# Tap matrices read from memory instead of built, and low weight parts made one stage earlier

## The chip, the cores and the metric

The kernel runs on one core of a Trainium2 chip. The metric is the device time of one execution in microseconds (us); a kernel's time is the median of several runs.

## The reference, cut to what matters

Two layers on a stream of 512 latent tokens of width 1024 (256 context tokens feed the first layer only). Layer 0 mixes tokens with gated linear attention, layer 1 with a convolution module; a SwiGLU block follows each.

```python
u = h @ w_in                                    # swiglu, hidden width 2816
y = (silu(u[..., :2816]) * u[..., 2816:]) @ w_out

u = h @ w_pw1 + b_pw1                           # conv_module: 1024 -> 2048
u = u[..., :1024] * sigmoid(u[..., 1024:])
u = depthwise_conv(u, w_dw) + b_dw              # 31 taps per channel
u = silu(layernorm(u, ln_g, ln_b))
y = u @ w_pw2 + b_pw2
```

Every sub-layer sees `rmsnorm(x) * (1 + scale) + shift`, and `x = x + gate * y` follows; the six vectors of a layer are `silu(c) @ w_mod[i] + b_mod[i]`.

## The kernel before

Activations lie with features on the 128 partitions and tokens along the free dimension, so a 1024-wide stream is 8 tiles of 128 x 512. Float32 products are made of three passes: a number is split in a high part (a cast to fp32r, on ScalarE) and a low part (the difference, on VectorE), and `mm3` adds high*high, high*low and low*high in PSUM. A weight block of 128 x 1024 arrives in a tile `wr` (3 buffers) from the SP queue, its high part goes to `wh` (4 buffers, L110) and its low part to `wl` (4 buffers, L111).

Activation tiles of 2 KB per partition come from a pool with a fixed number of buffers for each tag: `x` 8, `h` 16, `s` 36, `c` 4, `d` 4, `t` 3, `g` 4. A tile asked for by `bt(tag)` takes a buffer of its tag when an earlier tile of the tag has had its last reader.

The stages around the change, in order of time:

- The first feed-forward block, `ffn(0, ...)`. Its first product (`pairs`, 22 pairs of weight blocks) reads the 16 `h` tiles of its input. `evac` writes the 22 hidden blocks as high and low tiles: 36 `s`, 4 `c` and 4 `d`.

```python
tag = "s" if j < 18 else "c" if j < 20 else "d"
sT.append((bt(tag, F32R), bt(tag, F32R)))
```

- Its second product (`out_proj`) runs over 8 output blocks `m`, the last one in two halves of 256 tokens, and reads all 44 hidden tiles for each. After each half, `after2` calls `in2`: the norm of the half (`rstd_y`, `newton`, `spread`) and, for each of 8 feature blocks, `modulate`, which writes the 16 `h` tiles of the convolution's input.
- Beside the first product run jobs (`mod_jobs`, called by `step(n)`) that make the modulation vectors: load a block of `w_mod` into `wm` (one buffer), multiply and sum on VectorE (L229), add a bias on GpSimd (L233).
- The convolution module. `toeplitz` first builds 27 tap tiles on GpSimd (L1128) for three feature blocks (`PCH`) whose taps run on TensorE. Then 8 pairs of products (`pair_mm`, weights by `pair_load`) alternate with the taps: three lanes in an order written out by hand put taps on VectorE (L1088), on GpSimd with ScalarE (L1046, L1047) and on TensorE (L1152). The order of the SP queue is not written by hand.
- The second pointwise product, then the second feed-forward block.

Of the kernel before, what the change touches and what calls it, by code (L numbers as in the profile page):

```python
# [7 lines left out]
F32 = mybir.dt.float32  # L8
F32R = mybir.dt.float32r
# [7 lines left out]
ALU = mybir.AluOpType  # L17

P = 128
# [36 lines left out]
def hybrid_kernel(ctx: ExitStack, tc: tile.TileContext, t: dict):  # L56
# [29 lines left out]
    def bt(tag, dt=F32):  # L86
        if tag in "cd":
            return wide(tag, dt)[:, 2:514]
        return big.tile([P, 512], dt, tag=tag, bufs=NBUF[tag], name=nm(tag))
# [14 lines left out]
    def load_w(ap, n=1024, lo_eng=dve):  # L104
        return hilo(load_raw(ap, n), n, lo_eng)
# [111 lines left out]
    def mod_jobs():  # L217

        ij = [(0, j) for j in range(16, 48)] + [(1, j) for j in range(48)]

        def load(i, j):
            raw = wts.tile([P, 1024], F32, tag="wm", bufs=1, name=nm("wm"))
            sp.dma_start(raw, t["wmod"][i, j])
            return raw
        raw = load(*ij[0])
        yield
        for n, (i, j) in enumerate(ij):
            o = i * 48 + j
            dve.scalar_tensor_tensor(raw, raw, 1.0, sil, op0=ALU.mult, op1=ALU.mult, accum_out=dots[:, o:o + 1])  # L229
            if n + 1 < len(ij):  # L230
                raw = load(*ij[n + 1])
            if j % 8 == 7:
                pool.tensor_tensor(mod[i][:, j - 7:j + 1], dots[:, o - 7:o + 1],  # L233
                                   col(C_BMOD + o - 7, 8), op=ALU.add)
            yield

# [2 lines left out]
    def step(n):  # L239
        for _ in range(n):  # L240
            if next(jobs, 0) == 0:
                return
# [695 lines left out]
            if beside:  # L938
                beside(i)

    def ffn(i, h_, gt2, nx, after):
        sT = []

        def evac(j, po, c0, c1):
            n = c1 - c0
            if c0 == 0:
                tag = "s" if j < 18 else "c" if j < 20 else "d"
                sT.append((bt(tag, F32R), bt(tag, F32R)))
            hi, lo = sT[j]
            a = bt("t")  # L950
            act.activation(a[:, :n], po[0][:, :n], AF.Silu)
            dve.tensor_tensor(a[:, :n], a[:, :n], po[1][:, :n], op=ALU.mult)  # L952
            act.copy(hi[:, c0:c1], a[:, :n])  # L953
            dve.tensor_tensor(lo[:, c0:c1], a[:, :n], hi[:, c0:c1].bitcast(F32), op=ALU.subtract)

        pairs(f"wf{i}", HC, h_, evac, lambda i: step(3))
        r = resid(gt2)

        def ev2(m, p_, c0, c1):
            r(m, p_, c0, c1)  # L960
            nx.add(m, xs[m], c0, c1)

        out_proj(f"wo{i}", HC, sT, ev2, nx.tail, after)

# [14 lines left out]

    def after2(hf):  # L980
        if hf == 0:
            step(100)
            make_a(acol[:, 24:32], mod[1][:, 8:16], col(C_GMIX + 8, 8))
            make_a(acol[:, 32:40], mod[1][:, 32:40], col(C_GFFN + 8, 8))
        in2(hf)

    ffn(0, in1.h, mod[0][:, 40:48], n2, after2)


    HALF = WID // 2  # L990
# [128 lines left out]

    toep, ug, pe_ps, scr = {}, {}, {}, {}  # L1120

    def toeplitz(m, tag="s"):

        c = (m - PCH[0]) * 4 * NSH * NF
        for i in range(0, 4 * NSH, 4):
            tt = bt(tag)
            w = wph[:, c + i * NF:c + (i + 4) * NF]
            pool.tensor_tensor(tt.rearrange("p (a b) -> p a b", b=32), m32.unsqueeze(1).to_broadcast([P, 16, 32]),  # L1128
                               w.unsqueeze(2).to_broadcast([P, 16, 32]), op=ALU.mult)
            for j in range(4):  # L1130
                toep[m, (i + j) // NSH, (i + j) % NSH] = tt[:, j * P:(j + 1) * P]

# [171 lines left out]
        return r  # L1304

    def pair_load(i):
        return [load_w(t["wp1"][2 * i]), load_w(t["wp1"][2 * i + 1])]

    def pair_mm(u, c0, c1, ks=range(KC), po=None):
        po = po or [ps(), ps()]  # L1310
# [6 lines left out]
    def bias2(k):  # L1317
        act.activation(xs[k], xs[k], AF.Identity, bias=gb2[:, k:k + 1])
# [32 lines left out]
            ev3(m, p_, *halves[hf])  # L1351

    ev3 = closing(mod[1][:, 16:24], n3)
    m32 = cst.tile([P, 32], F32, name="m32")
    sp.dma_start(m32, t["m32"])
    bph = cst.tile([P, 4 * len(PCH)], F32, name="bph")
    sp.dma_start(bph, t["bph"])
    wph = bt("g")
    sp.dma_start(wph[:, :len(PCH) * 4 * NSH * NF], t["wph"])
    for m in range(KC):  # L1360
        if m in PCH:
            toeplitz(m)
        else:
            cv_new(m)
    uw = {0: pair_load(0), 1: pair_load(1)}
    prod = wts.tile([P, 1024], F32, tag="wm", bufs=1, name=nm("wm"))
# [2 lines left out]
    with tc.manual_schedule(engines={E.Activation, E.DVE, E.Pool, E.PE}):  # L1369
        pool_lane = pool_order()  # L1370
        dve_start, dve_lane = dve_order()
        warm(AF.Sigmoid)
        po.update({(i, h): pair_mm(uw[i], *h) for h, i in ((h0, 0), (h0, 1), (h1, 0))})
        evc(0, po[0, h0], *h0)
        mix(dve_start[0],
            at=[(0.4, lambda: evc(1, po[1, h0], *h0)), (0.7, lambda: uw.update({2: pair_load(2)}))])
        evc(0, po[0, h1], *h1)
        po[1, h1] = pair_mm(uw[1], *h1)
        po[2] = pair_mm(uw[2], 0, SEQ)
        mix(take(pool_lane, 5), dve_start[1], at=[(0.7, lambda: evc(1, po[1, h1], *h1))])  # L1380
        for p in range(1, 7):
            def evac():
                if p > 1:
                    need(ORD[p])
                    po[ORD[p + 1]] = pair_mm(uw[p + 1], 0, SEQ, range(4))

            def second():
                if p > 1:
                    pair_mm(uw[p + 1], 0, SEQ, range(4, KC), po[ORD[p + 1]])

            def load():
                if p + 2 < KC:
                    uw[p + 2] = pair_load(ORD[p + 2])
            at = [(0.04, evac), (0.25, load), (0.5, second)]
            if p >= 3:
                at += [(0.6, lambda: bias2(2 * p - 6)), (0.8, lambda: bias2(2 * p - 5))]
            if p == 3:
                at += [(SH[0], shift_sums), (SH[1], shift_bc), (SH[2], shift_copy)]
            if p >= 5:
                at += [(0.3, lambda: to_groups(ORD[p]))]  # L1400
            mix(take(pool_lane, PN[p - 1]), take(dve_lane, DN[p - 1]), at=at)
        mix(pe_lane(4), take(pool_lane, PN[6]), take(dve_lane, DN[6]),
            at=[(N6, lambda: need(6)), (N6, lambda: to_groups(6)), (0.3, lambda: load2(0)), (0.7, lambda: load2(1))])
        pe_store(4)
        mix(pe_lane(5), take(pool_lane, PN[7]), take(dve_lane, DN[7]),
            at=[(0.3, lambda: load2(4, "s")), (0.9, lambda: pe_back(4, dve))])
        pe_store(5)
        warm(AF.Silu)
        mix(pe_lane(6), pool_lane, dve_lane, at=[(0.1, lambda: load2(2)), (0.2, lambda: load2(3))])
        cv_new(6)  # L1410
        pe_out(6, 0, act)
        pe_out(6, 1, act)
        pool.tensor_tensor(cv[6][0:64], cv[6][0:64], ncb[0:64], op=ALU.add)
        ln_open()
        pe_out(6, 2, dve)
        pe_out(6, 3, dve)
        pe_back(5, act)
        ks = (1, 0, 2, 3, 4, 7, 5, 6)
        for k in ks:
            run(ln_sums(k, 0, k == ks[-1]))  # L1420
        b = [f for k in ks for f in ln_sums(k, 1, k == ks[-1])]
        run(take(b, S1))
        ln_stat(0)
        ln_bc(0)
        run(take(b, S2))
        lane = ln_lane(0)
        run(take(lane, 5))

        def rest():
            run(b)  # L1430
            run(lane)
            ln_stat(1)
        first = pw2(range(4), 0, {1: rest, BC: lambda: ln_bc(1)})
        load2(5, "s")
        lane = ln_lane(1)
        run(take(lane, L1))
        pw2_out(first, 0)
        run(lane)
        pw2_out(pw2((4, 5), 0), 0)
        pw2_out(pw2(range(4), 1), 1)  # L1440
        load2(6)
        load2(7)
        pw2_out(pw2((4, 5), 1), 1)
# [16 lines left out]
            (sp, act)[k // 2 % 2].dma_start(t["out"][k:k + 2, :, c0:c1].rearrange("k p c -> p k c"),  # L1460
                                            y.rearrange("p (k c) -> p k c", k=2))

    ffn(1, in3.h, mod[1][:, 40:48], n4, final)

# [14 lines left out]
def phases(w):  # L1481

    import numpy as np
    pad = NF * MID + NF - 1 - WID // 2
    wp = np.pad(w, ((pad, pad), (0, 0)))
    r, d, f = np.ogrid[:NF, :NSH, :NF]
    a = wp[NF * d + r - f + NF - 1].reshape(NF, NSH, NF, KC, 4, 32)[:, :, :, list(PCH)]
    return np.ascontiguousarray(a.transpose(0, 5, 3, 4, 1, 2)).reshape(P, -1)


def layout(x, c, ctx, c_ctx, w_mod, b_mod, norm_mix_g, norm_ffn_g, gla_w_in, gla_wa_f, gla_ba_f,
# [26 lines left out]
    tt = np.arange(512)  # L1518
    a["pmask"] = np.ascontiguousarray((np.arange(P)[:, None] > (tt % P)[None]).astype(f32))
    a["ident"] = np.eye(P, dtype=f32)  # L1520
    a["m32"] = np.ascontiguousarray(np.tile(np.eye(32, dtype=f32), (4, 1)))
    b = conv_b_dw[0].reshape(KC, 4, 32)[list(PCH)].reshape(-1, 32).T
    a["bph"] = np.ascontiguousarray(np.tile(b, (NF, 1)))
    a["wph"] = phases(conv_w_dw[0])
    a["wgo"] = _units(gla_w_out[0])
    a["wp1"] = _pairs(conv_w_pw1[0])
    a["wp2"] = _units(conv_w_pw2[0])
# [21 lines left out]
```

## Time and profile before

| | us |
|---|---|
| median of 3 runs | 1287.11 (1284.47 to 1287.29) |
| the profiled execution | 1287.67 |
| its span, from the first to the last instruction | 1285.7 |

The profile shows the one profiled execution. Times in it are counted from the start of the span. Busy time is that of instructions on an engine; TensorE's matmuls are pipelined, so their durations overlap. The granted clock is the share of TensorE's full speed that it had.

### The profile page before, as it was taken

Reading aid. Unit: us, or ns where it says so; the run is one execution under the profiler, and the core shown is the slowest. Engines: PE = TensorE matmul, PEld = TensorE weight load, DVE = VectorE, ACT = ScalarE, POOL = GpSimd, SP = SyncE. Lnnn points to the kernel's source line nnn. Section 1 sums busy time; section 2 is a strip of 40 time slices with the busy share of each in tenths; the row PEclk is TensorE's granted clock in tenths of the full one; section 3 lists DMA queues with packets and bytes.
Section 4 is the critical chain, followed back from the end, with each engine's and each line's share of the span. In section 5 each row is a group of like instructions: output and inputs, shape, how many; then the busy total and the mean of one; then the engine's idle time right before and its main releaser. Section 6 shows DMA issues by size and latency. Waiting matters only on the chain.

```text
span 1285.7 us, 17000 instructions
## 1 busy us (share of the span) xinstructions
PE 1234.1 (96%) x6692; PEld 1069.6 (83%) x6692; DVE 734.7 (57%) x1279; ACT 475.8 (37%) x748; POOL 226.9 (18%) x191
## 2 busy tenths in 40 slices
PE   8899899999899999999999699999999999999997
PEld 7678799898898888877888598889988888888886
DVE  2997976747775545545532889986733333332223
ACT  3245655443342222222222368855422222222220
POOL 0032211122200000000011859933000000000110
PEclk7999999999899999999999899999999999999999
DMA  7642542235456666556633123321143333333321
GB/s 277 223 132 74 164 147 83 83 99 149 141 167 196 193 186 196 194 166 205 195 112 101 50 66 95 117 85 65 55 128 99 97 95 95 93 95 100 93 72 66
DMA packets 54180, 162.34 MB, mean 126 GB/s; under 512 B 6226, under 2 KB 12242, under 8 KB 54100
## 3 DMA queue, kind: packets, MB, share of 16 engines
q1 hardware_dynamic: 52436, 159.16, 39.8%
q10 hardware_dynamic: 1664, 2.10, 0.5%
q8 instruction: 52, 0.85, 0.3%
q14 instruction: 28, 0.23, 0.1%
HBM read 157.83 MB, written 3.41 MB: 125 GB/s over the span
## 4 chain that ended last, share of the span: by engine, by line
PE 67%; DVE 16%; DMA 9%; issue 4%; ACT 3%; POOL 0%; DVEq 0%; ACTq 0%; POOLq 0%
PE pm L95 18%; PE pm L97 18%; PE pm L96 18%; DMA wm<-wmod 8%; DVE g L253 3%; DVE pa L1088 2%; DVE wl L111 2%; DVE wm L229 2%; PE pm L366 1%; PE pm L367 1%; PE pm L368 1%; ACT wh L110 1%; PE pa L620 1%; PE pm L527 1%; DVE pm L1088 1%
## 5 line engine op out<-in xcount | busy, mean ns | idle before, releaser
L97 PE MATMUL pm<-h,wl 128*128 128x512 f32 (+1 forms) x1008 | 373.3, 372 | 4.9 <-DVE wl L111 2.8
L96 PE MATMUL pm<-h,wh 128*128 128x512 f32 (+1 forms) x1008 | 372.1, 371 | 2.8 <-DVE h L199 2.8
L95 PE MATMUL pm<-h,wh 128*128 128x512 f32 (+1 forms) x1008 | 371.9, 372 | 0.2 <-ACT wh L110 0.2
L111 DVE TENSOR_TENSOR wl<-wr,wh 128x1024 fp32r<-128x1024 f32 (+1 forms) x176 | 224.6, 1280 | 256.9 <-ACT wh L110 255.0
L110 ACT CAST wh<-wr 128x1024 fp32r<-128x1024 f32 (+2 forms) x197 | 200.3, 1025 | 421.6 <-PE pm L96 398.8
L97 PEld LDWEIGHTS pm<-h,wl 128*128 128x128 f32 x1008 | 191.0, 190 | 39.2 <-DVE wl L111 4.4
L96 PEld LDWEIGHTS pm<-h,wh 128*128 128x128 f32 x1008 | 191.1, 190 | 35.2 <-DVE h L199 3.4
L95 PEld LDWEIGHTS pm<-h,wh 128*128 128x128 f32 x1008 | 190.1, 190 | 31.7 <-ACT wh L110 0.7
L95 PE MATMUL pm<-s,wh 128*128 128x512 f32 (+1 forms) x540 | 187.2, 347 | 1.1 <-ACT s L1271 1.1
L96 PE MATMUL pm<-s,wh 128*128 128x512 f32 (+1 forms) x540 | 186.8, 346 | 0.3 <-DVE s L278 0.2
L97 PE MATMUL pm<-s,wl 128*128 128x512 f32 (+1 forms) x540 | 186.0, 345 | 0.0
L229 DVE SCALAR_TENSOR_TENSOR wm<-wm,sil 128x1024 f32<-128x1024 f32 x80 | 102.0, 1275 | 129.1 <-DMA wm<-wmod 129.0
L885 POOL TENSOR_TENSOR g<-g,g 128x512 f32<-128x512 f32 (+1 forms) x31 | 39.8, 1283 | 488.4 <-ACT g L883 487.6
L96 PEld LDWEIGHTS pm<-s,wh 128*128 128x128 f32 x540 | 103.6, 192 | 13.1 <-DVE s L278 0.9
L95 PEld LDWEIGHTS pm<-s,wh 128*128 128x128 f32 x540 | 103.6, 192 | 13.2 <-ACT s L1271 1.3
L97 PEld LDWEIGHTS pm<-s,wl 128*128 128x128 f32 x540 | 103.6, 192 | 11.8
L111 POOL TENSOR_TENSOR wl<-wr,wh 128x1024 fp32r<-128x1024 f32 x21 | 53.1, 2541 | 198.7 <-ACT wh L110 198.7
L233 POOL TENSOR_TENSOR mod<-dots,cols 128x8 f32<-128x8 f32 x10 | 4.4, 443 | 277.6 <-DVE wm L229 277.6
L1088 DVE SCALAR_TENSOR_TENSOR pa<-s,cols,pa 128x503 f32<-128x503 f32 (+18 forms) x80 | 52.8, 701 | 0.6
L898 DVE SCALAR_TENSOR_TENSOR x<-pm,mod,x 128x256 f32<-128x256 f32 (+1 forms) x44 | 25.7, 601 | 47.5 <-PE pm L97 47.5
L953 ACT CAST s<-t 128x512 fp32r<-128x512 f32 (+1 forms) x40 | 23.1, 578 | 48.2 <-DVE t L952 48.2
L366 PE MATMUL pm<-wh,h 128*128 128x256 f32 x128 | 37.0, 289 | 0.0
(266 smaller groups left out, 1588.2 us busy)
## 6 DMA issues: line engine op xcount, KB each, us to landing
wr<-wf SPq DMA_DIRECT2D x88, 512.0 KB, 4.3
wm<-wmod SPq DMA_DIRECT2D x80, 512.0 KB, 3.7
wr<-wo SPq DMA_DIRECT2D x32, 512.0 KB, 3.7
wr<-wp SPq DMA_DIRECT2D x24, 512.0 KB, 3.9
s<-wmod SPq DMA_DIRECT2D x24, 256.0 KB, 5.5
wr<-wv SPq DMA_DIRECT2D x12, 512.0 KB, 4.1
wr<-wo SPq DMA_DIRECT2D x16, 384.0 KB, 3.3
wr<-wgo SPq DMA_DIRECT2D x8, 512.0 KB, 4.0
```

Source lines behind the costliest of these rows:

```text
L95: pe.matmul(out, wh, xh, start=start, stop=False)
L96: pe.matmul(out, wh, xl, start=False, stop=False)
L97: pe.matmul(out, wl, xh, start=False, stop=stop)
L110: act.copy(hi[:, :n], raw[:, :n])
L111: lo_eng.tensor_tensor(lo[:, :n], raw[:, :n], hi[:, :n].bitcast(F32), op=ALU.subtract)
L229: dve.scalar_tensor_tensor(raw, raw, 1.0, sil, op0=ALU.mult, op1=ALU.mult, accum_out=dots[:, o:o + 1])
L253: dve.scalar_tensor_tensor(junk, wt, 1.0, vec, op0=ALU.mult, op1=ALU.mult, accum_out=dsum[:, o:o + 1])
L366: pe.matmul(o, a, wh[:, w], start=k == 0, stop=False)
L885: pool.tensor_tensor(self.acc[:, c0:c1], self.acc[:, c0:c1], s[:, c0:c1], op=ALU.add)
L898: dve.scalar_tensor_tensor(xs[m][:, c0:c1], p_[:, :c1 - c0], gate[:, m:m + 1], xs[m][:, c0:c1], op0=ALU.mult, op1=ALU.add)
L953: act.copy(hi[:, c0:c1], a[:, :n])
L1088: dve.scalar_tensor_tensor(p_[:, lo:hi], u_sb[m][:, lo + s:hi + s], wcol(m, j), p_[:, lo:hi], op0=ALU.mult, op1=ALU.add)
```

## The change

- The 27 tap tiles are laid out on the host (`banded`) and loaded by the SP queue, nine for each of three feature blocks, at points inside the convolution stage, in place of 27 multiplications on GpSimd before it.
- Beside the second product of the first feed-forward block, `split_ahead(j)` takes each of the 16 weight blocks of the first pointwise product: two halves of 128 x 512 are loaded into `h` tiles, cast into `d` tiles on ScalarE, subtracted into `h` tiles on VectorE, and the low parts stored to DRAM. Output block `m` calls it for three of them. In the convolution, `pair_load` still loads the weights and casts the high part, and now reads the low part back from DRAM.
- The jobs for the modulation vectors go two to a pair of the first product (three before), one to an output block of the second, and the last eight, loaded into `wr`, to the second feed-forward block. Their bias is added on VectorE.

```diff
+            if (i, j) >= (1, 40):
+                raw = load_raw(t["wmod"][i, j])
             dve.scalar_tensor_tensor(raw, raw, 1.0, sil, op0=ALU.mult, op1=ALU.mult, accum_out=dots[:, o:o + 1])
-            if n + 1 < len(ij):
+            if n + 1 < len(ij) and ij[n + 1] < (1, 40):
                 raw = load(*ij[n + 1])
             if j % 8 == 7:
-                pool.tensor_tensor(mod[i][:, j - 7:j + 1], dots[:, o - 7:o + 1],
+                dve.tensor_tensor(mod[i][:, j - 7:j + 1], dots[:, o - 7:o + 1],
                                    col(C_BMOD + o - 7, 8), op=ALU.add)
...
-        pairs(f"wf{i}", HC, h_, evac, lambda i: step(3))
+        pairs(f"wf{i}", HC, h_, evac, beside)
...
         def ev2(m, p_, c0, c1):
             r(m, p_, c0, c1)
             nx.add(m, xs[m], c0, c1)
+            if beside2 and c0 == 0:
+                beside2()
...
         if hf == 0:
-            step(100)
...
-    ffn(0, in1.h, mod[0][:, 40:48], n2, after2)
+    def split_ahead(j):
+        raw = (bt("h"), bt("h"))
+        for i in range(2):
+            sp.dma_start(raw[i], t["wp1"][j][:, i * 512:(i + 1) * 512])
+        low_d[j] = drm.tile([P, 1024], F32, name=nm("low"))
+        for i in range(2):
+            hi, lo = bt("d", F32R), bt("h", F32R)
+            act.copy(hi, raw[i])
+            dve.tensor_tensor(lo, raw[i], hi.bitcast(F32), op=ALU.subtract)
+            left.append((low_d[j][:, i * 512:(i + 1) * 512], lo))
+
+    def beside1():
+        step(1)
+        m = n_ahead[0]
+        n_ahead[0] += 1
+        for o, lo in left:
+            sp.dma_start(o, lo.bitcast(F32))
+        left.clear()
+        for j in range(3 * m, min(3 * m + 3, 16)):
+            split_ahead(j)
+
+    ffn(0, in1.h, mod[0][:, 40:48], n2, after2, lambda i: step(2), beside1)
...
-    def toeplitz(m, tag="s"):
-        c = (m - PCH[0]) * 4 * NSH * NF
+    def toeplitz(m):
         for i in range(0, 4 * NSH, 4):
-            tt = bt(tag)
-            w = wph[:, c + i * NF:c + (i + 4) * NF]
-            pool.tensor_tensor(tt.rearrange("p (a b) -> p a b", b=32), m32.unsqueeze(1).to_broadcast([P, 16, 32]),
-                               w.unsqueeze(2).to_broadcast([P, 16, 32]), op=ALU.mult)
+            tt = bt("s")
+            sp.dma_start(tt, t["toep"][PCH.index(m), i // 4])
...
     def pair_load(i):
-        return [load_w(t["wp1"][2 * i]), load_w(t["wp1"][2 * i + 1])]
+        res = []
+        for j in (2 * i, 2 * i + 1):
+            raw = load_raw(t["wp1"][j])
+            hi = wts.tile([P, 1024], F32R, tag="wh", name=nm("wh"))
+            lo = wts.tile([P, 1024], F32R, tag="wl", name=nm("wl"))
+            act.copy(hi, raw)
+            sp.dma_start(lo.bitcast(F32), low_d[j])
+            res.append((hi, lo))
+        return res
...
+            if p <= len(PCH):
+                at += [(0.35, lambda: toeplitz(PCH[p - 1]))]
...
-    ffn(1, in3.h, mod[1][:, 40:48], n4, final)
+    ffn(1, in3.h, mod[1][:, 40:48], n4, final, lambda i: step(1))
```

## Rows read from the trace of the kernel before

**Rows 1.** The page, busy time of each engine (us, share of the span, instructions).

```profile
PE 1234.1 (96%) x6692; PEld 1069.6 (83%) x6692; DVE 734.7 (57%) x1279; ACT 475.8 (37%) x748; POOL 226.9 (18%) x191
```

**Rows 2.** Windows by stage: length, busy us and instructions of each engine, granted clock, DMA.

```profile
core 0: us, PE busy (x) PEld busy (x) DVE busy (x) ACT busy (x) POOL busy (x), PEclk, DMA share, GB/s
343.00:604.00 261.00, 257.28 (x1233) 216.22 (x1232) 150.74 (x229) 78.14 (x111) 3.43 (x7) 1.00 0.59 183
604.00:722.00 118.00, 112.87 (x562) 96.27 (x562) 51.17 (x64) 28.51 (x35) 22.84 (x20) 0.99 0.41 129
722.00:746.00 24.00, 17.19 (x115) 16.29 (x114) 21.68 (x35) 8.30 (x19) 19.84 (x25) 0.79 0.13 43
746.00:848.00 102.00, 101.22 (x603) 89.72 (x602) 95.13 (x124) 78.44 (x121) 83.71 (x70) 1.00 0.36 108
```

**Rows 3.** Waits of TensorE, 595 to 760 us: total, times, longest.

```profile
PE pa L170 <- DVE sm L190: 9.2, 2, 5.1
PE pm L96 <- DVE h L199: 2.8, 3, 2.3
```

**Rows 4.** Timeline of VectorE, steps of the norm, early and at the second product's end.

```profile
96.92 0.16 DVE L185 SCALAR_TENSOR_TENSOR sm<-sm 128x2 f32<-128x2 f32 x1
...
707.25 0.96 DVE L185 SCALAR_TENSOR_TENSOR sm<-sm 128x2 f32<-128x2 f32 x1
```

**Rows 5.** Groups on GpSimd, 700 to 745 us: count, busy us, mean ns, idle before.

```profile
L1128 POOL TENSOR_TENSOR s<-m,g 128x512 f32<-128x512 f32 x27 | 29.5, 1125 | 5.1 <-PE pm L96 5.1
```

**Rows 6.** Groups on VectorE, 744 to 848 us.

```profile
L1088 DVE SCALAR_TENSOR_TENSOR pa<-s,cols,pa 128x503 f32<-128x503 f32 (+18 forms) x80 | 52.8, 701 | 0.6
L111 DVE TENSOR_TENSOR wl<-wr,wh 128x1024 fp32r<-128x1024 f32 x16 | 25.1, 1602 | 4.1 <-ACT wh L110 4.1
```

**Rows 7.** Tile d, 580 to 725 us: min/median/max ns, first and last start.

```profile
L97 PE MATMUL pm<-d,wl x18: 282/393/402, 605.2 to 720.5; 128*128 128x512 f32 x14, 128*128 128x256 f32 x4
L953 ACT CAST d<-t x2: 622/623/624, 590.2 to 601.0; 128x512 fp32r<-128x512 f32 x2
L954 DVE TENSOR_TENSOR d<-t,d x2: 685/687/689, 593.2 to 603.8; 128x512 fp32r<-128x512 f32 x2
```

**Rows 8.** Tile h, 575 to 604 us.

```profile
L97 PE MATMUL pm<-h,wl x22: 388/389/499, 575.2 to 590.9; 128*128 128x512 f32 x22
```

**Rows 9.** Tile g, from 612 us.

```profile
L883 ACT ACTIVATE g<-x x7: 632/632/635, 615.4 to 697.6; 128x512 f32<-128x512 f32 x7
L1359 SPq DMA_DIRECT2D g<-wph x1: 383/383/383, 699.3 to 699.3; - x1
```

**Rows 10.** Tile bph, whole span.

```profile
L1357 SPq DMA_DIRECT2D bph<-bph x1: 430/430/430, 66.3 to 66.3; - x1
```

**Rows 11.** The page, DMA issues: count, KB each, median us to landing.

```profile
wm<-wmod SPq DMA_DIRECT2D x80, 512.0 KB, 3.7
s<-wmod SPq DMA_DIRECT2D x24, 256.0 KB, 5.5
x<-xT SPq DMA_DIRECT2D x8, 256.0 KB, 4.3
s<-ctxT SPq DMA_DIRECT2D x4, 256.0 KB, 4.6
scr<-s SPq DMA_DIRECT2D x3, 256.0 KB, 2.0
scr<-h SPq DMA_DIRECT2D x2, 256.0 KB, 4.6
```

**Rows 12.** Windows as in rows 2, short stretches about the second product's end and an early one.

```profile
714.00:718.00 4.00, 4.00 (x26) 4.00 (x25) 3.36 (x7) 1.85 (x3) 1.22 (x2) 0.66 0.02 4
730.00:742.00 12.00, 7.82 (x41) 7.53 (x42) 10.52 (x15) 1.31 (x3) 11.84 (x13) 0.57 0.13 43
15.00:31.00 16.00, 15.63 (x62) 13.29 (x60) 2.65 (x10) 2.02 (x3) 0.00 (x0) 0.51 0.72 247
7.00:15.00 8.00, 8.00 (x39) 6.07 (x40) 3.31 (x11) 4.39 (x9) 0.00 (x0) 0.91 1.03 358
```

**Rows 13.** Groups on VectorE by shape, 343 to 722 us.

```profile
L229 DVE SCALAR_TENSOR_TENSOR wm<-wm,sil 128x1024 f32<-128x1024 f32 x54 | 66.2, 1225 | 115.4 <-DMA wm<-wmod 115.2
L197 DVE SCALAR_TENSOR_TENSOR t<-x,acol,pa 128x256 f32<-128x256 f32 x19 | 8.4, 475 | 3.8 <-PE pa L170 3.7
```

More of the change, by code (lines that the diff above doesn't have):

```diff
@@ L939, in pairs, with ffn @@
                 beside(i)
-    def ffn(i, h_, gt2, nx, after):
+    def ffn(i, h_, gt2, nx, after, beside, beside2=None):
         sT = []
@@ L985, in after2 @@
         in2(hf)
-    ffn(0, in1.h, mod[0][:, 40:48], n2, after2)
+    bph = cst.tile([P, 4 * len(PCH)], F32, name="bph")
+    sp.dma_start(bph, t["bph"])
+    low_d = {}
+    left = []
+    def split_ahead(j):
[17 more added lines that the diff above has]
+            split_ahead(j)
+    n_ahead = [0]
+    ffn(0, in1.h, mod[0][:, 40:48], n2, after2, lambda i: step(2), beside1)
     HALF = WID // 2
@@ L1353, in hybrid_kernel @@
     ev3 = closing(mod[1][:, 16:24], n3)
[L1354 to L1359, printed above, removed]
     for m in range(KC):
-        if m in PCH:
-            toeplitz(m)
-        else:
+        if m not in PCH:
             cv_new(m)
@@ L1488, in phases, with banded @@
     return np.ascontiguousarray(a.transpose(0, 5, 3, 4, 1, 2)).reshape(P, -1)
+def banded(w):
+    import numpy as np
+    ph = phases(w).reshape(P, len(PCH), NSH, 4 * NF)
+    a = np.zeros((len(PCH), NSH, P, 4 * NF, 32), np.float32)
+    for p in range(P):
+        a[:, :, p, :, p % 32] = ph[p]
+    return a.reshape(len(PCH), NSH, P, SEQ)
 def layout(x, c, ctx, c_ctx, w_mod, b_mod, norm_mix_g, norm_ffn_g, gla_w_in, gla_wa_f, gla_ba_f,
@@ L1520, in layout @@
     a["ident"] = np.eye(P, dtype=f32)
-    a["m32"] = np.ascontiguousarray(np.tile(np.eye(32, dtype=f32), (4, 1)))
     b = conv_b_dw[0].reshape(KC, 4, 32)[list(PCH)].reshape(-1, 32).T
     a["bph"] = np.ascontiguousarray(np.tile(b, (NF, 1)))
-    a["wph"] = phases(conv_w_dw[0])
+    a["toep"] = banded(conv_w_dw[0])
     a["wgo"] = _units(gla_w_out[0])
```

## The prediction

> **What bounds the kernel now.** I read the page first: TensorE is busy 96% of the span, and no other engine over 57% [rows 1]. So time can only be won where TensorE stands still or runs slowly, and lost where the change makes it stand. The windows by stage [rows 2] show where that is: beside the first feed-forward block's first product TensorE is short of its window by 3.7 us in 261, in the convolution's main stretch by 0.8 us in 102; the weak stretch is 722 to 746, with 17.2 us busy of 24 at a granted clock of 0.79. The waits of TensorE name the reason [rows 3]: twice, 9.2 us in all (one of 5.1, the other so 4.1), it waits for the last step of the norm's reciprocal root (L190), and 2.8 us for a low part of the convolution's input (L199). The timeline shows why these are long: a step on two columns takes 0.16 us early in the kernel and 0.96 us at 707 us [rows 4], when GpSimd is building the 27 tap tiles, 29.5 us between 705 and 742 [rows 5]. In the convolution VectorE, busy 95.1 us of 102, is as full as TensorE [rows 2].
>
> **What the change takes away.** The tap tiles leave GpSimd, and the norm's steps go back to 0.16 us. Both waits for L190 go, 9.2 us, and most of the 2.8 us. TensorE also ran at clocks of 0.66 for 4 us and 0.57 for 12 us around these waits [rows 12], the lower of its two levels for part of each; 4 x 0.34 = 1.4 us and, of the 12 us less some 6 us of waits in them, 2.5 us are lost to it. VectorE loses the 12 subtractions of the first pointwise weights that lie in the convolution; the 16 of that form there (four are of other weights) take 25.1 us [rows 6], so 12 take 18.8. But TensorE has only 0.8 us of idle time there, so this is worth at most 0.8 us. If all that is added were hidden, the gain would be 9.2 + 2.8 + 1.4 + 2.5 + 0.8 = 16.7 us at most; I would count 13, since the second wait lies behind other VectorE work.
>
> **What it moves at no cost.** The modulation jobs: one takes 3.7 us to land [rows 11] and 1.23 us on VectorE [rows 13], 4.9 us. Three were 14.8 us against 261 / 22 = 11.9 us for a pair, and ran on into the second product; two are 9.9 us and fit. Eight go beside the second product and eight into the second feed-forward block, where a job of 4.9 us has a pair of 11.9 us. Without that cover a job costs its 4.9 us. The biases are ten instructions of two-digit width; nothing waits behind them.
>
> The 27 tap loads (7 MB) and the low parts read back (8.4 MB, 6.3 of it inside the convolution) go on the SP queue among the weight loads. The stretch moves 108 GB/s x 102 us = 11 MB now [rows 2]; with 13.4 more it needs 240 GB/s, and 358 was moved at 7 to 15 us [rows 12]. Pairs are loaded two ahead, 22 us, so I count nothing; if it were not hidden, one late pair would cost the landing of a load, 4 to 5 us.
>
> **What it adds, and where it runs.** This is the term that decides. `split_ahead` is called beside the second product, where ScalarE and VectorE have 90 and 67 us free [rows 2]. Its work would fit: 32 casts of 0.62 us and 32 subtractions of 0.69 us, by the rows of the same shape [rows 7]. But each cast writes a `d` tile. There are four buffers of `d`, and the hidden blocks 20 and 21 hold all four as high and low parts, written at 590.2 to 603.8 and read by TensorE for every output block until 720.5 [rows 7]. `h` tiles, which the loads need, come free only when the first product ends, about 591 [rows 8]. So no cast of the 32 has both its input and its buffer before the last matmul of the second product. The engines' order shows what is done then. The load of `wph` into a `g` tile waits for no data, and `g` lies unused before the squares at 615.4, yet it goes out at 699.3, after the `g` tiles that come before it in the program [rows 9]; a load with a buffer of its own, far behind in the program, went out at 66.3 [rows 10]. Buffers of one tag are given in program order. The same order puts the 16 `h` tiles of the convolution's input behind the 64 `h` tiles of the splits. So the splits stand between the second product and the convolution, with TensorE idle.
>
> The sum, on the times of the trace:
>
> - The last reader of `d` ends at 720.5 - 5.1 - 1.4 = 714.0, since the first wait and its slow clock go.
> - The first two blocks' inputs are there by then: four casts and a last subtraction, 4 x 0.62 + 0.69 = 3.2; 717.2.
> - A later block's loads get `h` buffers only when the block before it has taken its own, and in the SP queue they stand behind stores that wait for a subtraction. I take two blocks in flight: the queue issues the load behind the stores of the block two before it. Issues 0.43 each (of the rows' load of 430 ns [rows 10]), two of them; landing 4.6 (rows of 256 KB give 4.3 to 5.5 [rows 11]; the 4.6 has as few transfers beside it); two casts 1.24; one subtraction 0.69: 7.4 us for two blocks. Seven times: 51.8; 769.0.
> - The first four blocks' low parts are read back for the first two pairs. A read waits in the SP queue for its store to land, 2.0 to 4.6 us [rows 11], and the next block's load waits behind it. Four waits, two to a round of two blocks: 2 x 3.3 = 6.6; 775.6.
> - Then the input's first `modulate` (0.475 for the first step [rows 13], the second likewise): TensorE restarts at about 776.6, against 720.5.
>
> That is 56.1 us later. Of what TensorE lost before after 720.5, 4.1 + 2.8 + 2.5 = 9.4 us don't return. New are a slow start after the long stand, for which the early stretch at 0.51 over 16 us [rows 12] bounds the loss at 7.8 and the short waits at 730 give 2.5, and the first pair's pace, 8 x 0.95 us of `modulate` against some 5.8 us of matmuls; I take 4.5 + 2 = 6.5. Less the 0.8 in the convolution: 56.1 - 9.4 + 6.5 - 0.8 = 52.4 us. The profiled execution took 1287.67 us, 0.6 over the median; so 1340 on it and 1339 as a median.
>
> A page of the Trainium skill, "DMA: Bandwidth & Descriptors", section "Anatomy of one DMA", fits a transfer as 2.0 us plus its bytes at 436 GB/s, made for transfers issued by GpSimd; an estimate from it for 256 KB is 2.6 us. The rows say 4.3 to 5.5, and the measured rows decide; by the page the seven rounds would be 14 us shorter, and the kernel 38 us slower instead of 52.
>
> **The rivals.**
>
> *Pipelined.* The loads run far enough ahead that only VectorE paces the splits: 714.0 + 1.2 + 32 x 0.69 = 737.3, restart 738.3. By the same accounts (restart less 720.5, less 9.4, plus 6.5, less 0.8) that is 14 us slower, 1301. For it: 16 `h` buffers hold four blocks at four tiles each, and SP has nothing else to do. Against it: `wph`, which was not let past a tile whose turn had not come, and stores in the same queue. The rule on overlapping transfers with compute in the Trainium skill's "DMA: Bandwidth & Descriptors", section "Rules for kernel authors" (issue early, wait late, and the fixed cost is hidden), would give this case; here the early issue hangs on the buffers.
>
> *One by one.* The store of a block's first half gets ahead of the next block's load in the SP queue. Then each load goes out only after the first subtraction of the block before: 0.86 + 4.6 + 0.62 + 0.69 = 6.8 us for a block, 15 times 102 us, 714.0 + 3.2 + 102 = 819, with some waits for read-backs a restart at 823: 99 us slower, 1386.
>
> *Hidden.* The splits run beside the second product after all. Then only the gain is left: 13 us faster, 1274. What speaks for it is the free time of ScalarE and VectorE; it needs a `d` buffer some 100 us earlier than the rows of tile `d` show one. It decides from the point where all 16 blocks are through by about 730: each block that is not costs 1.4 us of VectorE at the least, so that ten blocks left over take the gain away.
>
> **How the numbers follow.** I give the forecast 0.5, pipelined 0.2, one by one 0.2, hidden 0.1. The predicted time is 1339. Its own range, from the bounds of landing (4.3 to 5.5, so 2 us down to 6 us up over seven rounds), read-back (2 x 2.0 to 4 x 4.6) and slow start (2.5 to 7.8), is 1332 to 1360. The range of 8 in 10 takes in pipelined and most of one by one: 1299 to 1388. What measurements of this kernel can tell from no change is about 0.3%, 4 us. Slower by more: 0.88, from the first three cases less a little for a pipelined case that gains more than I count; faster: 0.10; neither: 0.02.
>
> **What would show it.** After about 714, casts from `h` to `d` of 128 x 512 on ScalarE, and subtractions on VectorE, with waits for loads between them, until 740 to 820, and TensorE idle in that stretch with a low granted clock at its end. The norm's steps at 0.16 us, no L1128 on GpSimd, and a convolution stretch of about 102 us with VectorE less full. The number is wrong if casts to `d` appear before the last matmul that reads `d`, or if the convolution's input gets `h` buffers ahead of the splits; then the loads of the first low parts are what the first pair waits for. If the splits stand where I say but the time is far off, the order of loads and stores in the SP queue is what I have wrong.

## The result and the profile after

The changed kernel takes 1347.95 us (median of 4 runs, 1345.08 to 1350.06), the kernel before 1287.2 us beside it; the ratio is 1.0476 with a 95% interval of 1.0449 to 1.0502, 61 us slower. The forecast was 1339 us, 52 us slower, with a range of 1299 to 1388. The profiled execution took 1349.43 us with a span of 1347.6.

The page of the changed kernel: busy time of each engine, and TensorE's busy time and granted clock in 40 slices.

```profile
PE 1232.0 (91%) x6692; PEld 1069.0 (79%) x6692; DVE 721.0 (53%) x1305; ACT 494.8 (37%) x780; POOL 183.1 (14%) x154
...
PE   8899899999999999999991049999999999999997
...
PEclk7999999999999999999995569999999999999999
```

TensorE is busy for the same time as before [rows 1], 1232 us in place of 1234, in a span 61.9 us longer; the hole is in one place, the slices 22 to 24. Its waits from 590 to 900 us have one great row, where rows of 9.2 and 2.8 us stood before [rows 3]; of the waits for the norm's last step 1.6 us are left:

```profile
PE pm L95 <- ACT h L198: 77.6, 1, 77.6
PE pa L170 <- DVE sm L190: 1.6, 1, 1.6
```

It waits once, for 77.6 us, for the first high part of the convolution's input (`modulate`, L198). What stands before that `modulate` is seen in tile `d`, from 580 us (min/median/max ns, first and last start); L1005 and L1006 are the cast and the subtraction of `split_ahead`:

```profile
L1005 ACT CAST d<-h x32: 603/618/621, 709.9 to 791.6; 128x512 fp32r<-128x512 f32 x32
L1006 DVE TENSOR_TENSOR h<-h,d x32: 682/692/694, 710.7 to 792.3; 128x512 fp32r<-128x512 f32 x32
...
L97 PE MATMUL pm<-d,wl x18: 282/393/401, 601.4 to 710.0; 128*128 128x512 f32 x14, 128*128 128x256 f32 x4
```

The first cast starts at 709.86, when only the last two matmuls that read `d` (709.90 and 710.02) are still to start; but for these last 0.4 us no cast lies beside the second product. The work itself is 32 x 0.62 us and 32 x 0.69 us; the stretch is 83 us long, 709.9 to 793.0. The waits of the SP queue in it (709 to 793 us) say what fills it:

```profile
SPq L1014 <- DVE h L1006: 52.0, 22, 4.6
SPq L101 <- ACT wh L1344: 2.5, 1, 2.5
...
SPq L1345 <- DMA low<-h: 0.8, 1, 0.8
```

For 52.0 us the queue stands at a store of a low part (L1014), which waits for its subtraction. In the order of time, on SP and on ScalarE:

```profile
743.95 3.69 SPq L1014 DMA_DIRECT2D low<-h  x2
747.75 0.86 SPq L1001 DMA_DIRECT2D h<-wp  x2
748.70 5.36 SPq L1014 DMA_DIRECT2D low<-h  x2
754.11 0.42 SPq L1001 DMA_DIRECT2D h<-wp  x1
```

```profile
745.95 0.62 ACT L1005 CAST d<-h 128x512 fp32r<-128x512 f32 x1 [3.32 <-DMA h<-wp]
747.17 0.62 ACT L1005 CAST d<-h 128x512 fp32r<-128x512 f32 x1 [0.60 <-DMA h<-wp]
752.36 1.14 ACT L1005 CAST d<-h 128x512 fp32r<-128x512 f32 x2 [4.58 <-DMA h<-wp]
```

Two stores stand ahead of the load issued at 747.75, and the second of them can go only when the subtraction after the cast of 745.95 is done (it starts at 746.60 and takes 0.69). The loads land at 752.36, 4.6 us later. So there is one block in flight: a load, its casts, a subtraction, a store's issue, the next load. It is so from the sixth block on, whose load goes out at 732.29. The windows of the stretch and of what follows (length, busy us and instructions of each engine, granted clock, DMA):

```profile
709.00:793.00 84.00, 3.77 (x24) 3.29 (x23) 23.29 (x42) 23.11 (x40) 1.65 (x10) 0.53 0.67 227
793.00:800.00 7.00, 6.87 (x35) 6.59 (x35) 6.68 (x16) 4.00 (x9) 0.00 (x0) 0.57 0.14 51
800.00:910.00 110.00, 110.00 (x678) 98.68 (x678) 82.99 (x126) 80.55 (x129) 73.88 (x69) 1.00 0.63 223
```

Everything on TensorE's side is short after the stand: 7 us at a mean clock of 0.57 (its lower level, 1.2 GHz, until 799 us, then the full 2.4), then full.

### The profile page after: what moved, and what is told of

It is laid out like the page before. It is cut to its first block, busy times and chain, and to the rows that moved or that the text cites. A ratio compares the mean times of both kernels' runs of the same rounds, so it can differ in the third digit from the quotient of the medians.

```text
span 1347.6 us, 17236 instructions
## 1 busy us (share of the span) xinstructions
PE 1232.0 (91%) x6692; PEld 1069.0 (79%) x6692; DVE 721.0 (53%) x1305; ACT 494.8 (37%) x780; POOL 183.1 (14%) x154
## 4 chain that ended last, share of the span: by engine, by line
PE 75%; DVE 11%; DMA 6%; issue 4%; ACT 3%; SPq 1%; POOL 1%; DVEq 0%; ACTq 0%; POOLq 0%
PE pm L96 21%; PE pm L95 21%; PE pm L97 21%; DMA h<-wp 4%; DVE g L256 2%; DVE wl L111 1%; DMA wm<-wmod 1%; PE pm L370 1%; PE pm L371 1%; PE pm L369 1%; ACT wh L110 1%; PE pa L623 1%; PE pm L530 1%; ACT d L1005 1%; DVE h L1006 1%
## 5 line engine op out<-in xcount | busy, mean ns | idle before, releaser
L95 PE MATMUL pm<-h,wh 128*128 128x512 f32 (+1 forms) x1008 | 371.8, 372 | 77.9 <-ACT h L198 77.6
L110 ACT CAST wh<-wr 128x1024 fp32r<-128x1024 f32 (+2 forms) x181 | 184.3, 1024 | 472.9 <-PE pm L96 468.3
L111 DVE TENSOR_TENSOR wl<-wr,wh 128x1024 fp32r<-128x1024 f32 (+2 forms) x160 | 198.6, 1243 | 236.9 <-ACT wh L110 235.0
L231 DVE SCALAR_TENSOR_TENSOR wm<-wm,sil 128x1024 f32<-128x1024 f32 x72 | 91.8, 1275 | 110.7 <-DMA wm<-wmod 110.6
L1006 DVE TENSOR_TENSOR h<-h,d 128x512 fp32r<-128x512 f32 x32 | 21.5, 691 | 58.9 <-ACT d L1005 58.7
L1005 ACT CAST d<-h 128x512 fp32r<-128x512 f32 x32 | 19.5, 618 | 60.9 <-DMA h<-wp 60.0
```

The source lines that it names most:

```text
L95: pe.matmul(out, wh, xh, start=start, stop=False)
L110: act.copy(hi[:, :n], raw[:, :n])
L111: lo_eng.tensor_tensor(lo[:, :n], raw[:, :n], hi[:, :n].bitcast(F32), op=ALU.subtract)
L1005: act.copy(hi, raw[i])
L1006: dve.tensor_tensor(lo, raw[i], hi.bitcast(F32), op=ALU.subtract)
```

## The experiments

**The parts one by one.** The first question was whether the stand is all that was lost, and what the two other parts are worth. The tap tiles alone, on the kernel before, loaded at the points inside the convolution where the change puts them:

```diff
-            tt = bt(tag)
-            w = wph[:, c + i * NF:c + (i + 4) * NF]
-            pool.tensor_tensor(tt.rearrange("p (a b) -> p a b", b=32), m32.unsqueeze(1).to_broadcast([P, 16, 32]),
-                               w.unsqueeze(2).to_broadcast([P, 16, 32]), op=ALU.mult)
+            tt = bt("s")
+            sp.dma_start(tt, t["toep"][PCH.index(m), i // 4])
```

> The kernel before, with the 27 tap tiles loaded from memory and nothing else of the change. Theory (GpSimd's building slowed the norm's steps on VectorE, and TensorE waited): both waits for L190 (9.2 us) and most of the slow clock around them go, 13 us faster, about 1274 us; the norm's steps at 0.16 us. Rival (what was waited for lies behind other work, and 7 MB more of loads crowd the convolution): within 4 us of 1287.

Measured: 1268.0 us (1264.3 to 1269.17) against 1286.56 for the kernel before; ratio 0.9852, 0.9817 to 0.9887, or 19 us faster (15 to 24). Of TensorE's waits between 595 and 760 us this is the one left, and the norm's step that took 0.96 us [rows 4] is back at 0.16:

```profile
PE pm L96 <- DVE h L199: 0.4, 1, 0.4
```

```profile
704.28 0.16 DVE L185 SCALAR_TENSOR_TENSOR sm<-sm 128x2 f32<-128x2 f32 x1
```

The theory holds; the 13 us that were counted were too few, and the bound of 16.7 lies inside the interval. The two profiled executions show where the time is: from the second product's first matmul to the convolution's first it is 122.9 us in place of 129.7, and from there to the first matmul of the layer norm's sums 117.9 in place of 127.7. That is 16.6 us; another 1.9 lie in the first product, which ends before any tap tile was built, and are taken up under the next run.

The page "GPSIMD Engine Reference" of the Trainium skill, section "Specifications", says that GpSimd's access to SBUF is shared with VectorE and that instructions of VectorE in a two-port mode or with two SBUF inputs contend for it; this pair of runs agrees, with 0.96 us beside GpSimd's multiplications and 0.16 us without them. In the kernel before, two steps of `modulate` show it side by side: L197, with one input in PSUM, takes its usual 0.47 us, and L199, with both in SBUF, 1.13 in place of 0.47:

```profile
724.12 0.47 DVE L197 SCALAR_TENSOR_TENSOR t<-x,acol,pa 128x256 f32<-128x256 f32 x1
724.51 1.13 DVE L199 SCALAR_TENSOR_TENSOR h<-t,mod,h 128x256 fp32r<-128x256 f32 x1
```

L183, a step of the norm with a single input, is slow there too (1.01 us in place of 0.17); whether it runs in a two-port mode no run shows.

The jobs alone, on the kernel before:

```diff
-        pairs(f"wf{i}", HC, h_, evac, lambda i: step(3))
+        pairs(f"wf{i}", HC, h_, evac, beside)
...
-            step(100)
...
-    ffn(0, in1.h, mod[0][:, 40:48], n2, after2)
+    ffn(0, in1.h, mod[0][:, 40:48], n2, after2, lambda i: step(2), lambda: step(1))
...
-    ffn(1, in3.h, mod[1][:, 40:48], n4, final)
+    ffn(1, in3.h, mod[1][:, 40:48], n4, final, lambda i: step(1))
```

> The kernel before, with only the modulation jobs respread (two to a pair, one to an output block, eight in the second feed-forward block, biases on VectorE). The changed kernel ended the first product some 4 us earlier. Theory: three jobs to a pair held back VectorE's writing of the last hidden blocks, so this part alone gives 3 to 4 us, about 1283 us. Rival: it gives nothing (what the prediction counted), 1287 us, and the 4 us come from elsewhere.

Measured: 1286.43 us (10 runs, 1283.73 to 1290.35); ratio 1.000, 0.9978 to 1.0022. In the medians this is nothing, as the prediction had counted, and the theory's 3 to 4 us lie outside the interval. The profiled executions say otherwise. From its first matmul on `h` to the second product's first on `s`, the first product takes 245.7 us in the kernel before, 243.8 with the tap tiles alone, and 241.8 or 241.9 in all seven kernels with the jobs spread anew. In the kernel before TensorE has this row of waits there (340 to 604 us); with the tap tiles alone it is 1.6 us, and in the seven it is gone:

```profile
PE pm L97 <- DVE wl L111: 2.8, 2, 2.0
```

So in the executions that were profiled the first product is 3.9 us shorter with the jobs spread anew. Why ten runs do not show it in the median is open: of the kernel before only one execution, of 1287.67 us, was profiled, and others may wait less there.

Both of these, without the splits:

```diff
-        for o, lo in left:
-            sp.dma_start(o, lo.bitcast(F32))
-        left.clear()
-        for j in range(3 * m, min(3 * m + 3, 16)):
-            split_ahead(j)
...
     def pair_load(i):
...
+        return [load_w(t["wp1"][2 * i]), load_w(t["wp1"][2 * i + 1])]
```

> The changed kernel without the splits, their stores and their reading back: low parts of the first pointwise weights are made on VectorE in the convolution, as before. Theory (all that was lost is the splits' stand): the gains of the two other parts add up, 13 + 4 us, about 1270 us. Rival (loads from memory or the respread jobs cost time somewhere): above 1280 us.

Measured: 1264.62 us (1263.4 to 1269.94); ratio 0.9839, 0.9801 to 0.9877. So the splits cost the changed kernel 1347.95 - 1264.6 = 83 us, and their stretch in its trace is 83 us long. The tap tiles with and without the jobs differ by 3.4 us in the median (1268.0 and 1264.62), within the spread of either.

**The buffer.** The changed kernel with one tag changed:

```diff
-            hi, lo = bt("d", F32R), bt("h", F32R)
+            hi, lo = bt("h", F32R), bt("h", F32R)
```

> The changed kernel with one word changed: the cast's tile has tag h, not d. Theory (no d buffer is free until the last matmul that reads d, and that alone puts the splits behind the second product): casts and subtractions now lie beside the second product, TensorE doesn't stand, and the time is that of the change without the splits or up to 1 us less, 1268 to 1271 us. Rival (the work doesn't fit beside the second product: transfers, the SP queue or VectorE hold up the output blocks): above 1285 us.

Measured: 1264.54 us (1262.1 to 1271.58); ratio 0.9845, 0.9795 to 0.9896. The whole stand is gone by a tag. The casts, from line L1005 of this kernel, lie beside the end of the first product and the second, and between 590 and 830 us TensorE waits 0.5 us in all the rows of its waits:

```profile
L1005 ACT CAST h<-h x32: 616/621/625, 578.8 to 668.5; 128x512 fp32r<-128x512 f32 x32
```

```profile
PE pm L1254 <- DVE d L1198: 0.5, 1, 0.5
```

This kernel and the one without the splits take the same time, and both are faster than the kernel before: hidden, the splits cost nothing and win nothing that the medians can tell. In the profiled executions the convolution, up to the layer norm's sums, takes 115.8 us with `h` and 117.9 without the splits, so some 2 us may be won. In the convolution (730 to 830 us) they take VectorE from 94.9 to 78.6 us busy, while TensorE is at 98.2 and 99.5 of 100 us with either. The first two rows are of the kernel without splits, the next of the one with `h`:

```profile
705.00:730.00 25.00, 24.63 (x205) 24.39 (x205) 20.30 (x49) 12.79 (x25) 2.54 (x10) 1.00 0.23 79
730.00:830.00 100.00, 98.24 (x571) 86.20 (x571) 94.91 (x130) 76.74 (x118) 85.23 (x73) 1.00 0.54 182
```

```profile
730.00:830.00 100.00, 99.46 (x584) 87.60 (x583) 78.59 (x119) 74.92 (x118) 76.29 (x73) 1.00 0.68 241
```

**What sets a block's price.** The stretch of the splits was forecast at 61.6 us (714.0 to 775.6) and is 83. First, whether it goes by the block:

```diff
-        for j in range(3 * m, min(3 * m + 3, 16)):
+        for j in range(3 * m, min(3 * m + 3, 8)):
...
-            sp.dma_start(lo.bitcast(F32), low_d[j])
+            if j in low_d:
+                sp.dma_start(lo.bitcast(F32), low_d[j])
+            else:
+                dve.tensor_tensor(lo, raw, hi.bitcast(F32), op=ALU.subtract)
```

> The changed kernel with only the first 8 of 16 weight blocks split ahead; for the other 8 pair_load subtracts on VectorE as before. Without splits the time was 1264.6 us, with 16 it is 1348: 83 us, 5.2 us a block. Theory (each block pays for itself, one load behind the other): about 8 x 5.2 = 42 us over 1264.6, some 1306 us. Rival (a fixed cost, such as a cold TensorE clock or the first read-backs, makes up most): above 1325 us, or below 1290 if the blocks pile up only late.

Measured: 1308.45 us (1301.86 to 1310.28); ratio 1.0169, 1.0126 to 1.0212. 44 us over 1264.6, 5.5 us a block: it goes by the block. Its casts run from 710.5 to 747.5, and in that time the SP queue stands at stores for 22.7 us:

```profile
SPq L1014 <- DVE h L1006: 22.7, 14, 4.3
```

Then the stores, by leaving them out; the low parts are made but used nowhere, and the convolution makes its own:

```diff
-        for o, lo in left:
-            sp.dma_start(o, lo.bitcast(F32))
         left.clear()
...
     def pair_load(i):
...
+        return [load_w(t["wp1"][2 * i]), load_w(t["wp1"][2 * i + 1])]
```

> The changed kernel with the splits computed but their low parts neither stored nor read back (pair_load subtracts on VectorE as before). The SP queue then holds only loads one after the other. Theory (a block's load stands in the SP queue behind the store of the block before it, which waits for that block's subtraction): loads run ahead, VectorE's 32 x 0.69 us or the loads' rate pace the splits, TensorE stands some 25 to 30 us, about 1290 to 1297 us. Rival (the buffers given in program order hold the loads on the chip too): it still stands 70 us or more, above 1330 us.

Measured: 1299.46 us (1293.8 to 1300.98); ratio 1.0095, 1.0059 to 1.0131. 48 us under the changed kernel, 35 over the one without splits; 2 us above the range that was expected, and far from the rival. The 32 casts now run from 706.3 to 734.4, and VectorE is busy 25 of 30 us: the pace of its subtractions. Leaving the stores out also gives back the low parts' `h` buffers at once; the next run keeps the stores.

```profile
L1005 ACT CAST d<-h x32: 614/619/622, 706.3 to 734.4; 128x512 fp32r<-128x512 f32 x32
```

```profile
706.00:736.00 30.00, 3.43 (x20) 2.77 (x18) 25.12 (x44) 23.18 (x39) 3.91 (x9) 0.58 0.86 304
```

Last, whether it is the stores' place in the queue or their bytes: the same stores from GpSimd's queue.

```diff
-            sp.dma_start(o, lo.bitcast(F32))
+            pool.dma_start(o, lo.bitcast(F32))
```

> The changed kernel with the stores of the low parts issued by GpSimd's queue in place of SP's; the same bytes move. Theory (the order in the SP queue is what makes a block wait for the one before): the loads run ahead of the stores, held only by read-backs of the first four blocks and by h buffers that stores give back, a stand of 35 to 50 us, 1300 to 1317 us. Rival (the bytes of the stores, not their place in the queue, slow the loads): as the changed kernel, above 1335 us.

Measured: 1320.39 us (1316.99 to 1328.53); ratio 1.0292, 1.024 to 1.0345. That lies between the two theories, outside the range of either. The trace splits it. The SP queue's waits (703 to 762 us) are now for read-backs, and in the second part of the stretch the DMA engines are full:

```profile
SPq L1345 <- DMA low<-h: 17.6, 3, 6.9
SPq L1001 <- DVE h L1006: 12.6, 16, 1.4
```

```profile
704.00:729.00 25.00, 1.80 (x13) 1.39 (x12) 6.99 (x17) 7.52 (x13) 4.47 (x8) 0.58 0.79 272
729.00:761.00 32.00, 0.29 (x1) 0.28 (x1) 16.46 (x25) 15.12 (x27) 12.65 (x25) 0.50 1.00 378
```

The first four blocks take 25 us, 17.6 of them at read-backs that wait for a store to land. The other twelve take 32 us, 2.7 us a block against some 5.2 in the changed kernel (730.5 to 793.0), at 378 GB/s and a DMA share of 1.00: half a megabyte in and half out for each. So by the traces the place in the queue is worth about 26 of the 83 us (57 us remain without it), and bytes and read-backs together another 28 (29 us remain without stores); by the medians the two steps are 28 and 21 us. One thing is not separated: issued by GpSimd, the stores landed in 5.5 us in place of 3.5 (medians), and a read-back waits for its store, so part of the 57 us can be this queue's own.

## Why the prediction was right, and what in it was wrong

**Where the work would run: right.** That casts into `d` cannot start before the last matmuls that read `d`, and that the convolution's input queues behind the splits, was read from the rows of tile `d` and from the order of the `g` tiles; the trace shows the first, and one changed tag takes the whole stand away, as the theory said. The "hidden" case is what that one tag would have given: 1264.5 us, against 1274 foreseen for it. One reason is that the gain was counted too small: the discount from 16.7 to 13 was not borne out, and of the 12 us in [rows 12] TensorE is busy for 7.8, so that the waits took 4.2 and not 6, and the lower clock cost some 3.4 us and not 2.5.

**The end of the second product** was put at 714.0 and came at 710.0. From its first matmul to the last that reads `d` it takes 122.7 us in place of 129.4: 6.7 us less, where 6.5 were counted. The other 3.9 us are those of the first product above. The prediction put them at nothing, though it had read that TensorE is 3.7 us short there.

**The first two blocks** were to be done 3.2 us after that, with their inputs there; it took 5.7, from 710.0 to 715.7. Only the first block's loads had gone out early, at 577.8, before the first product ended; the second block's went out at 709.57. The loads' row (first and last start), and the SP queue in order of time:

```profile
L1001 SPq DMA_DIRECT2D h<-wp x32: 328/422/752, 577.8 to 788.2; - x32
```

```profile
709.57 0.90 SPq L1001 DMA_DIRECT2D h<-wp  x2
```

**The rounds: the step that was wrong.** "Two blocks in flight" gave 51.8 us for 14 blocks; measured are 793.0 - 715.7 = 77.3 us, 5.5 a block. Up to the fifth block loads do go out two blocks at a time, but from the sixth on a load stands behind a store of the block just before it, which is the rival "one by one". That rival had the order right for most blocks and the price too high: 6.8 us a block, with two issues and a landing of 4.6. The loads landed in 3.8, below the bounds of 4.3 to 5.5:

```profile
h<-wp SPq DMA_DIRECT2D x32, 256.0 KB, 3.8
```

With this landing and only the first half's issue it is 0.43 + 3.8 + 0.62 + 0.69 = 5.5. [rows 11] had a nearer row than those that were taken: 512 KB into `wm`, 3.7 us.

**The read-backs** were counted at 6.6 us. In the changed kernel the SP queue waits 0.8 us for them; it was held longer by the stores that stood in front. With the stores on GpSimd's queue it waited 17.6 us for them: the term was real, but hidden.

**After the stand** the stretch from TensorE's restart to the layer norm's sums is 792.7 to 910.4, 117.7 us; before, counted as in the prediction from 720.5, it ends at 848.4, 127.9. That is 10.2 us back, where 9.4 - 6.5 + 0.8 = 3.7 were counted. The kernel with the tag `h` does the same work there without a stand in 115.8, so the slow start and the first pair's pace cost about 2 us and not 6.5. The rest is in what the kernel before had lost there, 12 us against the 10.2 counted.

**The sum, and luck.** The restart came at 792.7 in place of 776.6. Too little was counted for the rounds (25.5) and the first two blocks (2.5), 28 us; too much for the end of the second product (4.0), the read-backs (6.6), the step to the restart (1.3) and what follows the stand (6.5), 18 us. The difference is the 9.6 us between 52.4 and the 62.0 measured. The place and the cause of the stand were foreseen; that the size came within 10 us is luck, since the term that decides it was 28 us short.

**What was moved at no cost** held as far as the medians tell: the jobs alone change nothing in them, and the tap loads and the read-backs beside the convolution, 223 GB/s in place of 108, leave TensorE full.

**The estimate by the Trainium skill** of 2.6 us for a load of 256 KB ("DMA: Bandwidth & Descriptors", section "Anatomy of one DMA") is under the 3.8 us that these loads took, as under the rows of before; the 38 us that it gave are farther off than the 52. The stores that GpSimd issued, the kind of transfer that its fit is made for, landed in 5.5 us here, with the DMA engines full beside most of them. The rule on early issue of the same page of the Trainium skill (section "Rules for kernel authors") is what the kernel with the tag `h` shows: there the loads go out early and TensorE's wait is gone. What stood against it here was the buffer, not the transfer.

What stays open is how the order of the SP queue comes about, store by store; that it costs about 26 us of the 83 is shown by one run, with GpSimd's later landings in it, and why the fifth block still goes with the fourth and the sixth does not was not tried.

## What to carry to other kernels

Work placed beside a stage runs there only if each tile that it writes has a buffer free in that stage: list the holders of the tag and their last readers before counting idle engines. A store in the same queue as the loads turned a stream into one block at a time here, since it waits for the result and the next load waits behind it; another queue gave part of that back, until the DMA engines were full. And where TensorE is full, taking work off a second full engine won 2 us at most, while steps of 0.96 us in place of 0.16 on the way to TensorE were most of the 19 us that the tap tiles won.

## What the runs showed of the hardware

- A VectorE step on two columns takes 0.16 us alone and 0.96 us beside GpSimd's multiplications of 128 x 512; in the kernel before that made TensorE wait 9.2 us and run at its lower clock around the waits. A step on 128 x 256 with both inputs in SBUF went from 0.47 to 1.13 us, one with an input in PSUM stayed at 0.47.
- After a stand of 77.6 us TensorE ran 7 us at a granted clock of 0.57 and was at 1.00 in the next window; about the wait of 4.1 us in the kernel before it was at 0.57 over 12 us, 7.8 of them busy [rows 12]. The long stand did not cost more clock than the short wait.
- Loads from memory and stores to it together reached 378 GB/s at a DMA share of 1.00; loads alone 358 [rows 12].
